# A batch-norm matmul on one core: the last column tile stored in sixteen blocks of one chunk, and the outputs of the fourth and fifth tiles moved forward

## The chip, the cores and the metric

One NeuronCore of a Trainium2 chip. The metric is the device time of one execution in microseconds (us). A profile shows one execution; its span is some 2 us shorter than the time. The granted clock in the views is the share of the full TensorE clock that was let through (1.00 is full speed). A ratio between two kernels is the mean time of one kernel's fast runs over the mean of the other's from the same rounds, so it is not quite the ratio of the medians quoted beside it.

## The reference

```python
def setup_inputs():
    batch, m, k, n = 16, 512, 1024, 768
    return {"x": randn(batch, m, k), "weight": randn(k, n),
            "gamma": ones(n), "beta": zeros(n), "eps": 1e-5}

def reference(x, weight, gamma, beta, eps):
    y = np.matmul(x, weight)
    mean = np.mean(y, axis=(0, 1), keepdims=True)
    var = np.var(y, axis=(0, 1), keepdims=True)
    y_norm = (y - mean) / np.sqrt(var + eps)
    return (gamma * y_norm + beta).astype(np.float32)
```

All is float32; y has 8192 rows and 768 columns. The statistics of a column need all its 8192 rows, so no element of a column can be stored before the last matmul of that column.

## The kernel before

The 768 columns are six tiles of 128. Tiles 0 to 2 are handled together (partly as rows, source line 179, "row matmuls" below), and tiles 3, 4 and 5 one after the other with transposed y (line 189, "y matmuls"). The text calls tiles 3, 4 and 5 the fourth, fifth and last tile. The rows are 16 chunks of 512. The program is emitted from a list of events with model times: what stands earlier in that list comes earlier in its engine's order. The engines then wait for each other by data only. TensorE writes its results to PSUM tiles; ScalarE or VectorE copies them to SBUF tiles (a "keep" where y itself is copied), and the SP queue stores output tiles to HBM by DMA.

The parts that the change touches:

```python
    def norm(nt, c, eng):              # y * scale + shift, in place, bf16, 128x512
        ...                            # ScalarE, VectorE (line 320) or GpSimd
    def turn_y(nts, m0, tiles):        # queue `tiles` transposes of 128x128 per column tile
        o_ps = psum.tile([P, tiles, len(nts), P], bf16, tag="b")
        ...
                turns.append(((nts, m0), o_ps[:, s, a], y(nt, c)[:, i * P:(i + 1) * P]))
    def turn_one():                    # one is emitted after each y matmul
        _, dst, src = turns.pop(0)
        seq(nc.tensor.transpose(dst, src, ident))
    def out_copy(nts, m0, eng, late=False):
        while any(k == (nts, m0) for k, _, _ in turns):
            turn_one()                 # what is left is emitted here, in a row
        ...                            # PSUM -> SBUF by ScalarE (line 349) or VectorE (line 351)
    def store(nts, m0, tiles): ...     # DMA to HBM from the SP queue

    def outputs(nt, t0, step):         # fourth and fifth tile: eight blocks of two chunks
        for b in range(C // 2):
            tb = t0 + step * b
            for i in range(2):
                at(tb - 1.4 + 0.5 * i, norm, nt, 2 * b + i, "act" if tb < tr + 2.0 else "dve")
            at(tb, turn_y, (nt,), 2 * b * CH, 2 * RT)
            at(tb + 2.2, out_copy, (nt,), 2 * b * CH, "act")
            at(tb + 2.3, store, (nt,), 2 * b * CH, 2 * RT)

    def last_outputs(nt, t0):          # nine blocks: 1, 1, then 2 chunks each
        blocks = [((0,), "v", "act"), ((1,), "v", "act"), ((2, 3), "gg", "dve"), ((4, 5), "vv", "act")]
        blocks += [((c, c + 1), "vv", "dve" if c % 4 == 2 else "act") for c in range(6, C, 2)]
        ...
    for nt in range(GA, NT):
        for c in range(EARLY, C):
            for jws in halves:
                unit(nt, c, MM_US / 2 + (0.12 if nt == GA else 0.17), jws)   # eight y matmuls a chunk
        at(pe + 0.55, finish, nt)      # aggregate, sqrt, reciprocal, scale, shift
        if nt == GA:
            outputs(nt, S + 40.0, 2.2)
        elif nt < NT - 1:
            outputs(nt, max(pe + 4.0, S + 55.0), 2.0)
        else:
            last_outputs(nt, pe + 3.0)
```

Of the kernel before, what the change touches and what calls it, by code (L numbers as in the profile page):

```python
# [10 lines left out]
def kernel(  # L11
# [36 lines left out]
    CH = 512  # L48
    RT = CH // P
    C = M // CH  # L50
# [312 lines left out]
    def at(t, fn, *args):  # L363
        events.append((t, len(events), fn, args))
# [6 lines left out]
    for kind, n, *n1 in order:  # L371
# [8 lines left out]
        m0 = n * rows  # L380
# [15 lines left out]
    pe = 0.0  # L396
# [12 lines left out]
    def unit(nt, c, span, jws=range(JW)):  # L409
        nonlocal pe  # L410
        pe = max(pe, arrive[c * RT + RT - 1])
        at(pe, mm, nt, c, jws)
        pe += span
        if jws[-1] == JW - 1:
            at(pe + 0.2, bn, nt, c)
            at(pe + 1.0, keep, nt, c)
# [12 lines left out]
    pe = max(pe, arrive["w", 2])  # L429
# [17 lines left out]
    S = pe  # L447
# [21 lines left out]
    def outputs(nt, t0, step):  # L469
# [7 lines that stand above are left out]

    def last_outputs(nt, t0):

        blocks = [((0,), "v", "act"), ((1,), "v", "act"), ((2, 3), "gg", "dve"), ((4, 5), "vv", "act")]  # L480
        blocks += [((c, c + 1), "vv", "dve" if c % 4 == 2 else "act") for c in range(6, C, 2)]
        tb = t0
        for chunks, by, eng in blocks:
            for c, who in zip(chunks, by):
                at(tb - (1.2 if who == "v" else 2.0), norm, nt, c, "dve" if who == "v" else "pool")
            m0, tiles = chunks[0] * CH, len(chunks) * RT
            at(tb, turn_y, (nt,), m0, tiles)
            at(tb + 0.5, out_copy, (nt,), m0, eng, True)
            at(tb + 0.6, store, (nt,), m0, tiles)
            tb += 0.5 * len(chunks)  # L490

    halves = [range(JW // 2), range(JW // 2, JW)]
    for nt in range(GA, NT):
        for c in range(EARLY, C):
            for jws in halves:
                unit(nt, c, MM_US / 2 + (0.12 if nt == GA else 0.17), jws)
        at(pe + 0.55, finish, nt)
        if nt == GA:
            outputs(nt, S + 40.0, 2.2)
        elif nt < NT - 1:  # L500
            outputs(nt, max(pe + 4.0, S + 55.0), 2.0)
        else:
            last_outputs(nt, pe + 3.0)

# [38 lines left out]
```

## Time and profile before

| | before |
|---|---|
| time, median of the first 3 runs | 223.67 us (223.32 to 224.12) |
| profiled span | 221.4 us |
| TensorE busy | 91% |
| last y matmul starts | 198.6 us |
| DMA engines full | 203.2 to 218.2 us |
| last data packet ends | 220.0 us |

One more view serves as a ruler: the list of one source line's instructions, which gives the first and last start of the row matmuls and of the y matmuls.

```profile
L179 PE MATMUL y_ps<-w_sb,xT_sb x320: 323/326/326, 24.8 to 120.0; 128*128 128x384 bf16 x160
L189 PE MATMUL y_ps<-xT_sb,w_sb x540: 273/387/632, 10.2 to 198.6; 128*128 128x512 bf16 x172, 128*128 128x256 bf16 x8
```

From 120.0 (last row matmul) to 198.6 (last y matmul) is 78.6 us, called the **stream**; from there to the end of the span is 22.8 us, the **tail**. The tail has the hand-over (the last statistics, the constants, the first blocks) and then the **drain**, in which the DMA engines are busy without a break.

### The profile page before, as it was taken

Reading aid. Unit: us, or ns where it says so; the run is one execution under the profiler, and the core shown is the slowest. Engines: PE = TensorE matmul, PEld = TensorE weight load, DVE = VectorE, ACT = ScalarE, POOL = GpSimd, SP = SyncE. Lnnn points to the kernel's source line nnn. Section 1 sums busy time; section 2 is a strip of 40 time slices with the busy share of each in tenths; the row PEclk is TensorE's granted clock in tenths of the full one; section 3 lists DMA queues with packets and bytes.
Section 4 is the critical chain, followed back from the end, with each engine's and each line's share of the span. In section 5 each row is a group of like instructions: output and inputs, shape, how many; then the busy total and the mean of one; then the engine's idle time right before and its main releaser. Section 6 shows DMA issues by size and latency. Waiting matters only on the chain.

```text
span 221.4 us, 3354 instructions
## 1 busy us (share of the span) xinstructions
PE 201.3 (91%) x1166; PEld 104.0 (47%) x1166; DVE 150.9 (68%) x260; ACT 117.5 (53%) x207; POOL 122.5 (55%) x145
## 2 busy tenths in 40 slices
PE   7669999999999999999999999999999999996510
PEld 3344555444545456465465544454444555555300
DVE  3222878897778888888634389778977568558930
ACT  2001553533554556465466217878879976858500
POOL 8897595964678689655069005996999300003000
PEclk9979999999999999999999999999999999997965
DMA  5999999999999999990000002898899998978995
GB/s 60 176 197 175 196 196 196 197 197 196 194 190 196 197 195 196 196 182 4 0 0 4 0 0 104 320 337 312 310 340 341 330 272 254 302 228 260 346 347 164
DMA packets 70049, 43.74 MB, mean 198 GB/s; under 512 B 3984, under 2 KB 69520, under 8 KB 70032
## 3 DMA queue, kind: packets, MB, share of 16 engines
q0 software_dynamic: 34624, 18.36, 60.6%
q1 hardware_dynamic: 35408, 25.18, 35.2%
q8 instruction: 9, 0.15, 0.3%
q14 instruction: 8, 0.07, 0.1%
HBM read 36.71 MB, written 25.17 MB: 280 GB/s over the span
## 4 chain that ended last, share of the span: by engine, by line
PE 84%; DMA 4%; DVE 3%; ACT 2%; issue 1%; POOL 1%; DVEq 0%; ACTq 0%; POOLq 0%
PE y_ps L189 52%; PE y_ps L179 23%; PE o_ps L336 7%; DMA ring<-in_x_dram 4%; DVE o_sb L351 1%; ACT o_sb L349 1%; POOL ring L155 1%; DVE y_sb L320 1%; ACT y_sb L315 1%; PE a_ps L262 1%; PE tot_ps L225 1%; ACT ring L349 0%; DVE xT_sb L167 0%; DVE stats L295 0%; ACT y_sb L298 0%
## 5 line engine op out<-in xcount | busy, mean ns | idle before, releaser
L189 PE MATMUL y_ps<-xT_sb,w_sb 128*128 128x512 bf16 (+1 forms) x540 | 133.0, 386 | 3.8 <-DVE xT_sb L167 1.9
L189 PEld LDWEIGHTS <-w_sb 128*128 128x128 bf16 x540 | 52.0, 97 | 69.7 <-issue 5.8
L295 DVE BATCH_NORM_STATS2 stats<-y_ps 128x6 f32<-128x512 f32 x66 | 45.0, 689 | 32.0 <-PE y_ps L189 31.8
L298 ACT CAST y_sb<-y_ps 128x512 bf16<-128x512 f32 x66 | 38.7, 586 | 52.2 <-DVE stats L295 49.5
L155 POOL DMA_DIRECT2D ring<-in_x_dram x72 | 45.3, 635 | 14.1 <-DVE xT_sb L167 7.4
L179 PE MATMUL y_ps<-w_sb,xT_sb 128*128 128x384 bf16 x320 | 53.1, 326 | 0.0
L336 PE MATMUL o_ps<-ident,y_sb 128*128 128x128 bf16 x264 | 45.5, 227 | 4.9 <-DVE y_sb L320 2.6
L167 DVE STREAM_TRANSPOSE xT_sb<-ring 128x1024 f32<-128x1024 f32 (+1 forms) x34 | 39.3, 1167 | 12.1 <-DMA ring<-in_x_dram 12.1
L205 POOL TENSOR_TENSOR sum<-sum,sq_sb 128x384 f32<-128x384 f32 x32 | 32.1, 1003 | 22.5 <-ACT sq_sb L201 21.3
L276 POOL TENSOR_TENSOR ring<-ring,sum 128x768 f32<-128x768 f32 x20 | 36.1, 1843 | 15.2 <-DVE ring L270 14.9
L179 PEld LDWEIGHTS <-xT_sb 128*128 128x128 bf16 x320 | 31.3, 98 | 21.6
L349 ACT CAST ring<-o_ps 128x1024 f32<-128x1024 bf16 (+1 forms) x28 | 25.8, 925 | 12.6 <-ACT y_sb L298 5.9
L208 DVE TENSOR_TENSOR sum<-y_ps,sum 128x384 f32<-128x384 f32 x40 | 21.8, 546 | 13.7 <-ACT sq_sb L201 13.1
L336 PEld LDWEIGHTS <-y_sb 128*128 128x128 bf16 x264 | 22.9, 101 | 9.9 <-DVE y_sb L320 6.0
L201 ACT ACTIVATE sq_sb<-y_ps 128x384 f32<-128x384 f32 x40 | 19.5, 493 | 13.1 <-PE y_ps L179 10.7
L214 ACT CAST y_sb<-y_ps 128x384 bf16<-128x384 f32 x40 | 19.0, 476 | 6.4 <-DVE sum L208 6.2
L270 DVE TENSOR_TENSOR ring<-y_sb,a_ps 128x768 f32<-128x768 bf16 x20 | 18.7, 938 | 0.0
L320 POOL TENSOR_SCALAR y_sb<-y_sb,scale,shift 128x512 bf16<-128x512 bf16 x2 | 1.7, 846 | 28.0 <-DVE shift L309 28.0
L315 ACT ACTIVATE y_sb<-y_sb,shift,scale 128x512 bf16<-128x512 bf16 x21 | 16.3, 816 | 0.0
L320 DVE TENSOR_SCALAR y_sb<-y_sb,scale,shift 128x512 bf16<-128x512 bf16 x43 | 16.1, 424 | 0.0
L148 PE MATMUL idle_ps<-idle_sb 128*128 128x512 bf16 x26 | 7.1, 441 | 1.2 <-DVE idle_sb L99 1.2
L142 POOL DMA_DIRECT2D w_sb<-in_weight_dram x12 | 6.1, 513 | 0.5 <-issue 0.2
(47 smaller groups left out, 36.3 us busy)
## 6 DMA issues: line engine op xcount, KB each, us to landing
ring<-in_x_dram POOLq DMA_DIRECT2D x56, 256.0 KB, 8.7
out_dram<-ring SPq DMA_DIRECT2D x32, 384.0 KB, 3.3
out_dram<-ring SPq DMA_DIRECT2D x16, 512.0 KB, 3.0
out_dram<-o_sb SPq DMA_DIRECT2D x7, 512.0 KB, 5.9
ring<-in_x_dram POOLq DMA_DIRECT2D x16, 128.0 KB, 5.2
w_sb<-in_weight_dram POOLq DMA_DIRECT2D x8, 96.0 KB, 4.5
w_sb<-in_weight_dram POOLq DMA_DIRECT2D x4, 192.0 KB, 5.1
out_dram<-o_sb SPq DMA_DIRECT2D x2, 256.0 KB, 4.7
```

The lines of the kernel that those rows point to most:

```text
L155: seq(nc.gpsimd.dma_start(x_bf[32 * i:32 * i + 32], src[:, :, KQ * i:KQ * (i + 1)]))
L167: seq(nc.vector.transpose(dst[:, half, :, jw0:jw1], src[:, :, jw0:jw1]))
L179: seq(nc.tensor.matmul(y_ps, xT[c][:, jw, s * P:(s + 1) * P, e], w_sb[:, jw, e, 0:NA], start=(jw == 0 and e == 0), stop=(jw == JW - 1 and ...
L189: seq(nc.tensor.matmul(y_ps, w_sb[:, jw, e, nt * P:(nt + 1) * P], xT[c][:, jw, q0 * QR:q1 * QR, e], start=(jw == 0 and e == 0 and q0 == 0) ...
L205: seq(eng.tensor_add(acc, acc, py.pop(("sq", c, s))))
L208: seq(nc.vector.tensor_add(sum1, py["row", c, s][:, 0:NA], sum1))
L276: seq(nc.gpsimd.tensor_add(o_sb, o_sb, sum1[:, None, :].to_broadcast([P, 2, NA])))
L295: seq(nc.vector.bn_stats(stats[:, nt, i, :], py[nt, c]))
L298: seq(nc.scalar.copy(y(nt, c), py.pop((nt, c))))
L320: seq((nc.vector if eng == "dve" else nc.gpsimd).tensor_scalar(y(nt, c), y(nt, c), scale[:, nt:nt + 1], shift[:, nt:nt + 1], op0=ALU.mult, ...
L336: seq(nc.tensor.transpose(dst, src, ident))
L349: seq(nc.scalar.copy(o_sb, src))
```

## The change

The intent: the fifth tile's outputs should be out of the way when the last tile is finished, and the last tile should leave in small equal blocks, with VectorE only normalising and ScalarE only copying. GpSimd has no part in it any more.

```diff
     def last_outputs(nt, t0):
 
-        blocks = [((0,), "v", "act"), ((1,), "v", "act"), ((2, 3), "gg", "dve"), ((4, 5), "vv", "act")]
-        blocks += [((c, c + 1), "vv", "dve" if c % 4 == 2 else "act") for c in range(6, C, 2)]
-        tb = t0
-        for chunks, by, eng in blocks:
-            for c, who in zip(chunks, by):
-                at(tb - (1.2 if who == "v" else 2.0), norm, nt, c, "dve" if who == "v" else "pool")
-            m0, tiles = chunks[0] * CH, len(chunks) * RT
-            at(tb, turn_y, (nt,), m0, tiles)
-            at(tb + 0.5, out_copy, (nt,), m0, eng, True)
-            at(tb + 0.6, store, (nt,), m0, tiles)
-            tb += 0.5 * len(chunks)
+        for c in range(C):
+            tb = t0 + 0.6 * c
+            at(tb - 1.2, norm, nt, c, "dve")
+            at(tb, turn_y, (nt,), c * CH, RT)
+            at(tb + 0.5, out_copy, (nt,), c * CH, "act", True)
+            at(tb + 0.6, store, (nt,), c * CH, RT)
 ...
         if nt == GA:
-            outputs(nt, S + 40.0, 2.2)
+            outputs(nt, S + 39.5, 2.0)
         elif nt < NT - 1:
-            outputs(nt, max(pe + 4.0, S + 55.0), 2.0)
+            outputs(nt, pe + 4.6, 1.85)
```

## The prediction

> **What bounds the kernel now.** I read the page first: TensorE busy 91%, and in slices the DMA row says that the last three slices are nothing but transfers. So I cut the span into windows: the stream of matmuls with its transposes, the hand-over, the drain, what is left.
>
> ```profile
> 166.00:199.00 33.00, 33.00 (x239) 17.75 (x237) 21.30 (x47) 26.10 (x37) 7.53 (x5) 1.00 0.90 288
> 199.00:203.20 4.20, 2.31 (x27) 1.70 (x25) 3.91 (x10) 3.65 (x6) 1.68 (x2) 0.85 0.81 243
> 203.20:218.20 15.00, 5.16 (x57) 3.70 (x54) 8.38 (x16) 3.98 (x5) 0.00 (x0) 0.73 1.14 344
> 218.40:219.90 1.50, 0.00 (x0) 0.00 (x0) 0.00 (x0) 0.00 (x0) 0.00 (x0) 0.50 0.08 23
> ```
>
> The columns are the window and its length, busy us of TensorE, its weight load, VectorE, ScalarE, GpSimd, then granted clock, DMA share and GB/s. TensorE has no gap up to 199.0, and the list of waits shows none for it from 120 to 199.1. From 203.2 to 218.2 the DMA engines run full at 344 to 348 GB/s and no compute engine does. 15.0 us x 344 GB/s is 5.16 MB; the last column tile is 8192 x 128 x 4 = 4.19 MB. The other MB is two blocks (0.52 MB each) of the fifth tile, as the timeline of the hand-over shows:
>
> ```profile
> 199.12 1.01 ACT L349 CAST ring<-o_ps 128x1024 f32<-128x1024 bf16 x1 [0.75 <-ACT y_sb L298]
> ...
> 201.23 1.93 ACT L349 CAST ring<-o_ps 128x1024 f32<-128x1024 bf16 x2
> 201.42 2.22 DVE L320 TENSOR_SCALAR y_sb<-y_sb,scale,shift 128x512 bf16<-128x512 bf16 x4
> 201.49 1.68 POOL L320 TENSOR_SCALAR y_sb<-y_sb,scale,shift 128x512 bf16<-128x512 bf16 x2 [27.96 <-DVE shift L309]
> ...
> 203.04 1.09 ACT L349 CAST o_sb<-o_ps 128x512 f32<-128x512 bf16 x2
> 203.67 12.07 SPq L354 DMA_DIRECT2D out_dram<-o_sb  x9
> ```
>
> ScalarE still copies two fifth-tile blocks ("ring") at 201.2 to 203.2, so the first last-tile copy ("o_sb") waits until 203.04 although its constants are ready at 201.4.
>
> The fourth window is odd: 1.5 us at 23 GB/s, a sixteenth of 347 or so: one DMA engine alone finishes late. The queue list of 202.4 to 204.6 shows why, I think:
>
> ```profile
> q1 hardware_dynamic: 1038, 0.52, 79.0%
> q8 instruction: 1, 0.02, 4.5%
> ```
>
> One 16 KB fetch of instructions lies just at the start of the drain (in the trace it starts at 202.87 and takes 1.59 us), and until about 204.5 the share is 1.08 instead of 1.15, again one sixteenth less. The engine that fetched starts 1.5 us late and, every engine having an equal share, ends 1.5 us late. So the end is **last matmul, then finish chain, then drain, then that straggler, then 1.5 us** of completion (219.9 to 221.4).
>
> **What the Trainium skill says.** "DMA: Bandwidth & Descriptors", Specifications: HBM gives a core about 358 GB/s; the trace's 347 in the drain agrees, so the drain can't be made faster, only started earlier and freed of other data. "Runtime: NRT & Kernel Launch", Instruction fetch mechanics: instructions are refilled in 16 KiB blocks (256 instructions) by a DMA queue of the sequencer, a cost "mostly hidden". The trace shows such packets (about 20 us apart lately), but the one at 202.87 seems not hidden. "GPSIMD Engine Reference", Specifications: GpSimd shares SBUF interfaces with VectorE in a 2-port mode; the trace agrees: four norms take 2.22 us (0.56 each) beside GpSimd's two and 1.38 us (0.35 each) later. "TensorE: Matmul & The Clock Gate", Part 1: an idle array falls to half clock; the windows show 0.50 from 202 to 205, transposes then at about 0.12 us.
>
> **The change part by part.** The order of instructions of the two builds shows what moves. Both have 64 + 17 against 64 transposes after the last y matmul: before, 17 of the fifth tile come after it, now none.
>
> 1. *Transposes before the last matmul.* Eight matmuls alone take 8 x 0.226 = 1.81 us (chain of waits: seven in 1.58); with eight transposes between, they follow each other at 0.2815, so a transpose costs 0.056. 17 x 0.056 = **+0.95 us** on TensorE's path: last matmul from 198.99 to 199.94.
>
> 2. *A stall at the fourth tile.* Its steps shrink too (2.2 to 2.0, start 0.5 earlier). The order shows its first transposes now after five matmuls of a unit, three matmuls (0.7 us) earlier than before. In the trace that transpose would be due at about 168.5, but the ScalarE norm that makes its data is the first of these two, ending about 169.1:
>
> ```profile
> 168.30 1.52 ACT L315 ACTIVATE y_sb<-y_sb,shift,scale 128x512 bf16<-128x512 bf16 x2
> 169.73 0.57 ACT L298 CAST y_sb<-y_ps 128x512 bf16<-128x512 f32 x1
> 170.19 1.53 ACT L315 ACTIVATE y_sb<-y_sb,shift,scale 128x512 bf16<-128x512 bf16 x2
> 171.62 0.57 ACT L298 CAST y_sb<-y_ps 128x512 bf16<-128x512 f32 x1
> 172.08 1.02 ACT L349 CAST ring<-o_ps 128x1024 f32<-128x1024 bf16 x1
> 172.99 1.53 ACT L315 ACTIVATE y_sb<-y_sb,shift,scale 128x512 bf16<-128x512 bf16 x2
> ```
>
> ScalarE is packed there, so TensorE waits: 0.6 us, and perhaps 0.1 for the norms at 172.99: **+0.7 us**, the term I trust least (0 to 1). Last matmul then 200.64.
>
> 3. *Overlap of fourth and fifth tile.* Three units now carry 52 transposes: TensorE 24 x 0.226 + 52 x 0.056 = 8.3 us; ScalarE 7 copies x 1.01 + 3 keeps x 0.59 = 8.8 us; seven blocks of 0.52 MB are 3.7 MB, 10.6 us of DMA at 347, which the ring of six blocks and the next, lighter units absorb. ScalarE falls behind by half a us; eight PSUM banks at three allocations per 2.7 us allow 7 us of life, and I count at most 6. **0**, with little to spare.
>
> 4. *Finish chain.* Before, 199.02 to 201.42, with one fifth-tile norm (0.31) between statistics and aggregation. That norm is now earlier: 2.10 us instead of 2.41, **-0.3 us**. Norms start at 202.75.
>
> 5. *First block.* Norm 0.35 (GpSimd is out of it), four transposes at half clock 0.48, copy about 0.55, some 0.1 of hand-overs: first store at about 204.2. From issue to the first byte takes 0.9 (the issue at 200.16 moves bytes from 201.1), so the drain starts at **205.2** instead of 203.2.
>
> 6. *Drain.* Only 4.19 MB: at 347 GB/s **12.1 us** (before 15.0). Each chunk is 0.76 us of DMA, against 0.35 of VectorE, at most 0.48 of TensorE, and about 0.58 of ScalarE (1.09 for two, beside GpSimd): supply outruns it. 512 KB or 256 KB blocks have the same 512-byte rows, so the rate should hold; the queue's issues (0.37 to 0.52 us each when not held back) fit. VectorE's four copies (4 x 1.22) vanish, which was hidden and is worth nothing. End of drain 217.3, was 218.2.
>
> 7. *Straggler.* The count of TensorE instructions ahead of the last tile is the same (row 2179 in both), so the fetch should come again about 1 us after its first transpose: 203.1 + 0.9 = 204.0, ending 204.9 at the undisturbed 0.95 us, just before the drain. Then no engine is late: **-1.5 us**. Last byte 217.3, was 219.9.
>
> Sum: 217.3 - 219.9 = -2.6 us, which gives 221.1; I put 221.2, since the fetch may still touch the drain.
>
> **Rivals.** *A stall takes the place of the hidden drain*: with ScalarE packed at 168 to 175 and again in the overlap, TensorE could lose 1.5 to 2 us instead of 0.7; then 222.0 to 222.5. For it: 26.1 of 33 us of ScalarE busy already. Against it: TensorE never waited there before. *The straggler stays*: the fetch is tied to something else and still hits the drain; then 222.6. For it: its margin above is 0.3 us. *No stall at all*: my placing of the transpose is 0.6 us off; then 220.4. *The small blocks starve the queue* because ScalarE alone copies (0.7 instead of 0.58 with waits): 16 x 0.7 = 11.2 us, still below 12.1; it would need 0.85 to cost 1.5 us. Unlikely.
>
> **Range and chances.** The plausible combinations run from 220.4 (no stall, no straggler) to 222.6; with 0.3 us of spread in the runs (223.32 to 224.12) I take 219.9 to 222.7. Faster by over 2% would need under 219.2: 1.3 us of gain beyond the best combination, 0.05. Slower by over 2% needs a lasting stall of over 4 us in the overlap: 0.02.
>
> **What would show it.** After the change: windows with the DMA share at or near 0 just before the drain; a drain of 12.1 us at 347 GB/s with no second phase at 23 GB/s; an instruction packet before the first store's bytes; the last y matmul at about 200.6, with 0.6 us of TensorE idle near 168.5 released by ScalarE's norm (if not, 199.9); GpSimd idle after 174; norms of 0.35. I am wrong if the first store comes later than 204.8, if the straggler is there again, or if DMA rate falls with 256 KB blocks.

## More of the kernel before

What lies ahead of 120 us, called the load phase (the loading of x and what runs beside it), differs between executions of one kernel by more than a microsecond. The stream and the tail do not contain it, so they show small effects that the total hides.

## The result, and the profile after

The changed kernel took 220.78 us (median of 4 runs, 220.42 to 221.63) against 223.56 us (4 runs). The ratio is 0.9878, with a 95% interval of 0.9842 to 0.9913. Two later sets of 6 runs gave 0.9914 each time. So the gain is between 0.9% and 1.2%, and inside the predicted range each time.

The windows of the changed kernel, cut as those of before (columns as there): the hand-over, the drain, what is left.

```profile
199.90:204.70 4.80, 2.08 (x22) 1.93 (x22) 4.39 (x14) 2.25 (x6) 0.00 (x0) 0.81 0.28 85
204.70:217.10 12.40, 3.36 (x46) 3.19 (x44) 2.77 (x9) 6.45 (x14) 0.00 (x0) 0.78 1.13 338
217.10:218.60 1.50, 0.00 (x0) 0.00 (x0) 0.00 (x0) 0.00 (x0) 0.00 (x0) 0.50 0.00 0
```

The drain is 12.4 us long instead of 15.0, and its data are the last tile's alone. After it nothing moves: the phase at 23 GB/s is gone, and only the 1.5 us of completion remain. Before the drain the DMA engines now stand nearly idle; the fifth tile's last bytes arrive at 201.3. The timeline of the hand-over shows one copier and one normaliser:

```profile
202.22 5.25 DVE L320 TENSOR_SCALAR y_sb<-y_sb,scale,shift 128x512 bf16<-128x512 bf16 x16
202.68 5.21 PEld L336 LDWEIGHTS <-y_sb 128*128 128x128 bf16 x64 [3.22 <-DVE y_sb L320]
202.68 5.38 PE L336 MATMUL o_ps<-ident,y_sb 128*128 128x128 bf16 x64 [2.71 <-DVE y_sb L320]
203.21 7.93 ACT L349 CAST o_sb<-o_ps 128x512 f32<-128x512 bf16 x16 [1.08 <-PE o_ps L336]
203.82 10.19 SPq L354 DMA_DIRECT2D out_dram<-o_sb  x16
```

Sixteen norms take 5.25 us (0.33 each), sixteen copies 7.93 us (0.50 each): both faster than the DMA, which needs 0.76 us for a chunk. The list of TensorE's waits and the ruler show what was paid for it:

```profile
PE o_ps L336 <- DVE y_sb L320: 2.7, 1, 2.7
PE o_ps L336 <- ACT y_sb L315: 0.5, 1, 0.5
...
L179 PE MATMUL y_ps<-w_sb,xT_sb x320: 323/326/326, 24.0 to 119.2; 128*128 128x384 bf16 x160
L189 PE MATMUL y_ps<-xT_sb,w_sb x540: 273/387/390, 10.1 to 199.6; 128*128 128x512 bf16 x172, 128*128 128x256 bf16 x8
```

(The waits are us in total, times, longest; the 2.7 us is the hand-over itself.) The stream is 80.4 us, 1.8 longer than before; the tail is 19.0 us, 3.8 shorter. Together 99.4 instead of 101.4: the last two tiles' stage gained 2.0 us. The two profiled spans differ by 2.8 us; the remaining 0.8 us is the load phase, which in this profile ended at 119.2 instead of 120.0 with the same instructions in it. That is luck, and no profile shows whether the other runs of the first set had it too. The later sets, with a gain of 1.9 us each (0.0086 of 223.5), agree with the stage.

### The profile page after: what moved, and what is told of

It reads as the page before. It is cut to its first block, busy times and chain, and to the rows that moved or that the text cites. A ratio compares the mean times of both kernels' runs of the same rounds, so it can differ in the third digit from the quotient of the medians.

```text
span 218.6 us, 3380 instructions
## 1 busy us (share of the span) xinstructions
PE 199.5 (91%) x1166; PEld 103.7 (47%) x1166; DVE 146.7 (67%) x258; ACT 121.2 (55%) x218; POOL 120.8 (55%) x143
## 4 chain that ended last, share of the span: by engine, by line
PE 82%; DMA 5%; ACT 4%; POOL 3%; issue 1%; DVE 1%; ACTq 0%; POOLq 0%
PE y_ps L189 51%; PE y_ps L179 24%; PE o_ps L336 6%; ACT o_sb L349 3%; DMA w_sb<-in_weight_dram 2%; DMA ring<-in_x_dram 2%; POOL w_sb L142 2%; POOL ring L155 1%; PE a_ps L262 1%; PE tot_ps L225 1%; ACTq L533 0%; ACT ring L349 0%; ACT y_sb L315 0%; DVE stats L295 0%; DVE mv L302 0%
## 5 line engine op out<-in xcount | busy, mean ns | idle before, releaser
L189 PEld LDWEIGHTS <-w_sb 128*128 128x128 bf16 x540 | 51.3, 96 | 68.5 <-issue 5.3
L336 PE MATMUL o_ps<-ident,y_sb 128*128 128x128 bf16 x264 | 43.1, 230 | 3.4 <-DVE y_sb L320 2.7
L276 POOL TENSOR_TENSOR ring<-ring,sum 128x768 f32<-128x768 f32 x20 | 36.1, 1833 | 15.3 <-DVE ring L270 15.1
L201 ACT ACTIVATE sq_sb<-y_ps 128x384 f32<-128x384 f32 x40 | 19.5, 494 | 11.1 <-PE y_ps L179 8.9
L214 ACT CAST y_sb<-y_ps 128x384 bf16<-128x384 f32 x40 | 19.1, 478 | 8.7 <-DVE sum L208 8.6
L148 PE MATMUL idle_ps<-idle_sb 128*128 128x512 bf16 x26 | 7.6, 462 | 1.2 <-DVE idle_sb L99 1.2
L349 ACT CAST o_sb<-o_ps 128x512 f32<-128x512 bf16 x16 | 7.9, 673 | 1.1 <-PE o_ps L336 1.1
```

What stands on the lines that cost most here:

```text
L189: seq(nc.tensor.matmul(y_ps, w_sb[:, jw, e, nt * P:(nt + 1) * P], xT[c][:, jw, q0 * QR:q1 * QR, e], start=(jw == 0 and e == 0 and q0 == 0) ...
L201: seq(nc.scalar.activation(sq_sb, py["row", c, s][:, 0:NA], AF.Square))
L276: seq(nc.gpsimd.tensor_add(o_sb, o_sb, sum1[:, None, :].to_broadcast([P, 2, NA])))
L349: seq(nc.scalar.copy(o_sb, src))
```

## The experiments

Eleven runs. The ruler for all of them, in us, from one profile each:

| version | stream | tail | both | ratio to before (95%) |
|---|---|---|---|---|
| before | 78.6 | 22.8 | 101.4 | 1 |
| changed, first set | 80.4 | 19.0 | 99.4 | 0.9878 (0.9842 to 0.9913) |
| changed again | 80.4 | 19.2 | 99.6 | 0.9914 (0.9882 to 0.9946) |
| changed again | 80.5 | 19.1 | 99.6 | 0.9914 (0.9894 to 0.9934) |
| only the last tile | 78.6 | 22.7 | 101.3 | 1.0014 (0.9981 to 1.0046) |
| only the fourth and fifth tile | 80.4 | 19.5 | 99.9 | 0.9905 (0.9868 to 0.9943) |
| changed, fourth tile back | 79.6 | 19.5 | 99.1 | 0.9906 (0.9860 to 0.9953) |
| the same again | 79.6 | 19.5 | 99.1 | 0.9881 (0.9858 to 0.9903) |
| before, fetch earlier | 78.6 | 21.3 | 99.9 | 0.9932 (0.9889 to 0.9974) |
| changed, fetch later | 80.4 | 20.8 | 101.2 | 0.9979 (0.9937 to 1.0021) |
| changed, fetch earlier | 80.4 | 18.9 | 99.3 | 0.9905 (0.9870 to 0.9940) |
| fourth tile back, idle matmuls | 79.6 | 18.8 | 98.4 | 0.9856 (0.9822 to 0.9890) |
| the same again | 79.5 | 18.8 | 98.3 | 0.9860 (0.9834 to 0.9886) |

### Which part of the change does it

The control, the changed kernel without an edit:

> The changed kernel once more, as the control for the runs beside it. Ratio to the kernel before 0.988 (0.985 to 0.991); 0.7 to 0.9 us of TensorE lost near 167 to 173 to ScalarE's norms; no second phase of the drain at 23 GB/s.

It came out at 0.9914, a little above what I wrote and at the upper end of the first set's interval (0.9913); stream and tail repeat to 0.2 us.

Only the last tile (the changed kernel with the old times for the two other tiles):

```diff
-            outputs(nt, S + 39.5, 2.0)
+            outputs(nt, S + 40.0, 2.2)
...
-            outputs(nt, pe + 4.6, 1.85)
+            outputs(nt, max(pe + 4.0, S + 55.0), 2.0)
```

> Only the first part of the change: the last tile in sixteen blocks of one chunk; fourth and fifth tile as before. Theory (the gain is the fifth tile leaving the drain, and the fetch of instructions leaving it): 17 transposes and two fifth-tile blocks still lie behind the last matmul, the drain still carries 5.2 MB from about 203.2, the fetch still falls into it; ratio to before 0.996 to 1.003. Rival (smaller blocks and ScalarE alone copying start the drain earlier and end it smoother): most of the gain, ratio 0.988 to 0.993.

Ratio 1.0014. The sixteen blocks alone gain nothing: stream and tail are those of before. The run with the fourth tile back (below) differs from this one only in the line of the fifth tile, and has 0.9906 and 99.1 us against 101.3: that one line makes the gain.

Only the other two tiles (the kernel before with the two new lines, the reverse of this edit):

> Only the second part: fourth and fifth tile further forward; the last tile in nine blocks, as before. Theory: nearly the whole gain, ratio 0.987 to 0.991, drain of 4.2 MB in 12.1 to 12.4 us, fetch of instructions before it, perhaps 0.2 us worse than both parts because GpSimd slows the first norms to 0.56 us. Rival (the sixteen blocks matter, the larger ones starve the queue at the start): ratio 0.994 or more, with gaps in the DMA share after the first store.

Ratio 0.9905, as good as the changed kernel within the intervals: the other two tiles' lines give the gain without the sixteen blocks. (The rival's 0.994 lies at the edge of the interval, 0.9943; the stretches decide, 99.9 us against 101.4.) The tail is 0.3 to 0.5 us longer than the changed kernel's, where I had written perhaps 0.2, and the drain takes 12.9 us (206.1 to 219.0), where I had written 12.1 to 12.4. The rival's sign is there too: for 0.5 us from 206.9 the DMA share is 0.11. But this gap lies ahead of the second store, which is one chunk in both kernels, so the larger blocks don't make it. GpSimd does slow the first norms, as expected:

```profile
203.66 2.21 DVE L320 TENSOR_SCALAR y_sb<-y_sb,scale,shift 128x512 bf16<-128x512 bf16 x4
203.74 1.67 POOL L320 TENSOR_SCALAR y_sb<-y_sb,scale,shift 128x512 bf16<-128x512 bf16 x2 [29.44 <-DVE shift L309]
```

Four norms in 2.21 us are 0.55 each, against 0.33. Yet the first store comes no later than in the changed kernel (4.15 us after the last y matmul started, against 4.14 to 4.35). The second is issued 0.70 us after the first, not 0.49, and its issue then takes 1.08 us, until 0.44 us after a fetch of instructions has ended. So most of the longer tail goes with the fetch, below; what GpSimd adds, one profile does not separate.

### The wait that the fourth tile brings

```diff
-            outputs(nt, S + 39.5, 2.0)
+            outputs(nt, S + 40.0, 2.2)
```

> The changed kernel with the fourth tile's outputs put back to their times before (start 40.0, step 2.2). Theory (TensorE waits 0.7 to 0.9 us for ScalarE's norms because the fourth tile starts 0.5 us too early): that wait is gone, last y matmul 0.7 to 0.9 us nearer to the tile's start, ratio to the changed kernel 0.996, to before 0.984. Rival (the wait comes back elsewhere, in the longer overlap of fourth and fifth tile where ScalarE has 4 blocks more to copy): same as the changed kernel, 0.988, with TensorE waiting on ScalarE at 180 to 192.

The total missed what I expected (0.9906 instead of 0.984), and the profiled execution was the slowest of its six (223.54 us; its load phase ended at 122.7). But the stream is 79.6 us, 0.8 shorter, and the wait on ScalarE's norm is gone from the list (120 to 206 us), which has one line left, the hand-over:

```profile
PE o_ps L336 <- DVE y_sb L320: 2.7, 1, 2.7
```

The longer overlap brought no new wait. So I ran it again, with the changed kernel and the last version on the same chip.

> The changed kernel a third time, so that the last two versions can be set against it on one chip. Ratio to before 0.988 to 0.992; 80.4 us from the last row matmul to the last y matmul, 19.0 to 19.3 from there to the end.

> The fourth tile's outputs at their old times, once more: in its first profile the fetch of instructions happened to collide with the first stores, and that profile was of its slowest execution. Theory: 79.6 us of matmul stream again (the wait of 0.8 us gone), tail 19.0 to 19.5 by how the fetch falls, so 0.5 to 0.8 us less than the changed kernel of this call. Rival (the 0.8 us come back in the tail): 99.4 us or more in both stretches together, total the same as the changed kernel.

The changed kernel came out as expected (0.9914, 80.5 and 19.1). With the fourth tile back it is again 79.6, and a tail of 19.5. Both together are 99.1 instead of 99.6: 0.5 of the 0.8 us arrive. (The total is 0.9967 of the changed kernel's, means 221.12 and 221.86 us, a difference of 0.7.) The other 0.3 us go with the second store, whose issue takes longer here (1.07 and 1.27 us against 0.74 to 0.97 in the three profiles of the changed kernel). What holds it is the next question.

### The fetch of instructions

In the kernel before, one DMA engine ended 1.5 us late, and the prediction put that down to a 16 KB fetch of instructions. In its trace 112 to 142 pairs of weight load and matmul lie between one 16 KB fetch and the next, 128 on average, and in all runs the last one starts after 1096 to 1118 weight loads. So I took the fetches to follow the count of pairs: some pairs more or fewer at the start of the program should shift all of them and touch nothing else.

The kernel before, with 40 pairs more (the waking matmuls that fill the wait for the first load):

```diff
-    WAKE = 26
+    WAKE = 20
...
         for _ in range(WAKE):
             seq(nc.tensor.matmul(idle_ps, idle_sb[:, 0:P], idle_sb, start=True, stop=True))
+        for _ in range(46):
+            seq(nc.tensor.matmul(idle_ps[:, 0:P], idle_sb[:, 0:P], idle_sb[:, 0:P], start=True, stop=True))
```

> The kernel before, with the waking matmuls recast as 20 long and 46 short ones: 40 more pairs of TensorE instructions ahead of everything, so each 16 KB fetch falls 40 pairs earlier; nothing else moves. Theory (the engine that ends 1.5 us late is the one that fetched at the start of the drain): the last fetch falls at about 197 to 199, the phase at 23 GB/s is gone, and from the last y matmul to the end it takes 21.3 us instead of 22.8; ratio to before 0.993 (0.990 to 0.996). Rival (one engine is slow by itself): 22.8 us and a ratio of 1.000, with the phase still there.

The fetch fell at 196.3, a little earlier than expected. The stream stayed at 78.6, and the tail became 21.3 us, as expected to the tenth. Its windows of hand-over, drain and rest:

```profile
199.90:204.40 4.50, 2.42 (x32) 1.69 (x30) 3.83 (x10) 3.57 (x6) 1.63 (x2) 0.99 0.78 236
204.40:219.60 15.20, 6.38 (x54) 5.21 (x52) 8.63 (x16) 4.05 (x6) 0.05 (x1) 0.50 1.14 344
219.60:221.20 1.60, 0.00 (x0) 0.00 (x0) 0.00 (x0) 0.00 (x0) 0.00 (x0) 0.50 0.03 7
```

The drain is as long as before (15.2 us: it still carries two blocks of the fifth tile), but the phase at 23 GB/s after it is gone. The ratio is 0.9932. That the late engine was late because of the fetch is shown by this run: only the waking matmuls were changed, and what came out of place was the fetch.

The opposite: the changed kernel with 20 pairs fewer, so that the fetch falls into the drain.

```diff
-    WAKE = 26
+    WAKE = 6
```

> The changed kernel with 6 waking matmuls instead of 26: 20 pairs fewer, so the last fetch falls some 1.7 us later, into the drain. Theory: a phase of 1.0 to 1.5 us at 23 GB/s comes back at the end, and last y matmul to end takes 20.2 to 20.7 us instead of the 19.0 to 19.2 of the changed kernel. Rival: 19.1, no such phase. The colder start can move the whole by up to 1 us either way, so the verdict is taken from that stretch and not from the total; total 0.990 to 0.999.

The tail grew to 20.8 us, a little more than I had written, and the total to 0.9979, which gives back most of the gain. But the phase at 23 GB/s at the end is only 0.8 us long. The rest was lost inside the drain, in a way that I had not expected:

```profile
207.20:209.40 2.20, 2.20 (x29) 1.52 (x30) 2.20 (x8) 2.20 (x5) 0.00 (x0) 1.00 1.14 338
209.40:210.40 1.00, 1.00 (x13) 0.65 (x12) 0.56 (x2) 1.00 (x4) 0.00 (x0) 1.00 0.12 27
210.40:220.60 10.20, 0.02 (x1) 0.00 (x0) 0.00 (x0) 3.35 (x7) 0.00 (x0) 0.68 1.11 335
220.60:221.40 0.80, 0.00 (x0) 0.00 (x0) 0.00 (x0) 0.00 (x0) 0.00 (x0) 0.50 0.08 23
```

For 1.0 us in the middle nearly all DMA engines stand still (share 0.12), although ScalarE has copied blocks ready. The timeline of the store queue in that run shows one issue that takes 2.25 us, where its neighbours take 0.5:

```profile
207.86 2.25 SPq L354 DMA_DIRECT2D out_dram<-o_sb  x1
```

The fetch in this run lasts from 208.00 to 209.71. The issue ends 0.4 us after it. The same interval appears where a fetch meets the first stores: the second store's issue ends 0.43 us after the end of the fetch in the changed kernel's first profile (204.62, 205.05), and 0.43 to 0.46 in its two others, in both runs with the fourth tile back and in the run of only the two tiles. So a fetch seems to do two things: it holds its own engine, and it can hold a store's issue until 0.4 us after its own end; if too little is queued by then, the other fifteen engines run dry. In the kernel before, an issue was held as well (203.67, for 1.72 us), but blocks of the fifth tile were still queued and the DMA engines went on (342 GB/s from 204.5 to 206), so only the first effect shows as lost time.

Two limits. Not every issue during a fetch is held: the changed kernel's first store (203.82, 0.37 us) is not, nor is a store of the fifth tile in the run above (196.94, 0.37 us). And issues are also long with no 16 KB fetch near, as the one at 215.76 in this run (1.08 us). So the times alone would not show it; the next run, which moves the fetch away from the second store, does. How the issue comes to wait is not visible in a trace.

The changed kernel with the 40 pairs more of the first edit:

> The changed kernel with the same recast waking matmuls as the other run (40 pairs more), nothing else. Theory (the fetch at the first stores stretches the second issue and so delays the drain): fetch near 198, second issue about 0.4 us, last y matmul to end 18.6 instead of 19.1; ratio to before 0.986 to 0.989. Rival (the second issue is always long): 19.1 us.

The fetch fell at 196.4, again earlier than expected. The second issue took 0.44 us, as expected. Here it is beside that of the changed kernel's first profile (line 356 is line 354 of the other):

```profile
204.31 0.74 SPq L354 DMA_DIRECT2D out_dram<-o_sb  x1
205.86 0.44 SPq L356 DMA_DIRECT2D out_dram<-o_sb  x1
```

But the tail is 18.9, not 18.6: the collision had cost only 0.1 to 0.3 us in the changed kernel, less than I had thought. The stretch from the first store's issue to the end of the span shows it best: 14.7 us here, 14.8 where the second issue takes 0.74 or 0.76 us, 15.0 at 0.97, and 15.1 and 15.3 at 1.07 and 1.27 with the fourth tile back. The ratio, 0.9905, does not tell this from the changed kernel.

The two runs with the fetch moved also say what the change is worth apart from it. With the fetch out of the way in both kernels, stream and tail together take 99.9 us before and 99.3 us after (mean times 221.9 and 221.3 us): 0.6 us. So of the 2.0 us that the change gains, about 1.4 come from the fetch no longer falling into the drain, and 0.6 from the rest. (These are one profile each and means of six runs; the intervals of the two ratios overlap.)

### A version that beats both

The fourth tile back at its old times, and 28 short idle matmuls after the last y matmul, while TensorE waits anyway. They are meant to keep its clock up, and to make the fetch fall ahead of the first stores.

```diff
+    def fill(n):
+        idle_ps = psum.tile([P, CH], f32, tag="b")
+        for _ in range(n):
+            seq(nc.tensor.matmul(idle_ps[:, 0:P], ident, ident, start=True, stop=True))
...
-            outputs(nt, S + 39.5, 2.0)
+            outputs(nt, S + 40.0, 2.2)
...
+            at(pe + 3.2, fill, 28)
             last_outputs(nt, pe + 3.0)
```

> The changed kernel with the fourth tile back at its old times and 28 short idle matmuls of TensorE after the last y matmul, which keep its clock up and pull the fetch of instructions ahead of the first stores. Theory: 79.6 us from the last row matmul to the last y matmul (80.4 in the changed kernel), then 18.3 to 18.7 to the end (19.0 to 19.2): the second store is issued in about 0.4 us instead of 0.74 to 1.07. Ratio to before 0.983 (0.980 to 0.986). Rival (stretching of the second issue has nothing to do with the fetch): 19.1 us, ratio 0.986 to 0.988.

> The version with the fourth tile back and the 28 idle matmuls, once more, against the changed kernel on the same chip. Theory: 98.4 us in both stretches together against 99.5, so a total 0.9 to 1.3 us below the changed kernel (ratio of the two 0.994 to 0.996) and 0.985 of before. Rival (the earlier difference was the luck of the load phase): ratio of the two within 0.002 of 1.

Both runs agree: stream 79.6 and 79.5, tail 18.8 (0.1 more than the upper end of what I wrote), the second issue 0.43 and 0.44 us, the granted clock 1.00 through the first transposes. The ratio to before is 0.9856 and 0.9860; to the changed kernel 0.9937 (means 220.46 and 221.86 us). That is 1.4 us, a little more than I wrote, of which 1.3 show in stream and tail. The edit does two things to the tail. The fetch now falls at 197.9, and from the first store's issue to the end it is 14.7 us, as in the run with the fetch earlier. The clock matters less: the first store is issued 4.14 or 4.15 us after the last y matmul in all profiles of kernels with sixteen blocks and the fifth tile moved in which the granted clock was 1.00 over the first 1.5 us of transposes. These include one of the changed kernel and one with the fourth tile back, without idle matmuls; it is 4.24 us at a clock of 0.56 and 4.35 at 0.50. So the clock's share is 0.1 to 0.2 us, in those executions where it was low.

## Why the prediction was right, point by point

The number (221.2) lies between the three medians of the changed kernel (220.78, 221.59, 221.80), and the predicted gain of 1.1% between the measured 0.9% and 1.2%. By its steps:

1. *Transposes ahead of the last matmul, +0.95.* Measured 1.0: the stream without the stall is 79.6, that of before 78.6.
2. *The stall at the fourth tile, +0.7.* Measured 0.8 (80.4 against 79.6). It was where it was said to be, counted from the last row matmul: this profile runs 0.8 us ahead. In the changed kernel's timeline the first of those transposes waits for ScalarE's norm:

```profile
166.52 1.29 PE L189 MATMUL y_ps<-xT_sb,w_sb 128*128 128x512 bf16 x5
168.33 0.23 PE L336 MATMUL o_ps<-ident,y_sb 128*128 128x128 bf16 x1 [0.52 <-ACT y_sb L315]
168.40 0.39 PE L189 MATMUL y_ps<-xT_sb,w_sb 128*128 128x512 bf16 x1
...
172.62 0.39 PE L189 MATMUL y_ps<-xT_sb,w_sb 128*128 128x512 bf16 x1
173.02 0.23 PE L336 MATMUL o_ps<-ident,y_sb 128*128 128x128 bf16 x1
```

   There are 0.52 us at 168, and another 0.2 at 172.6, where the next transpose follows 0.40 us after its matmul instead of 0.23. The "perhaps 0.1" of the prediction was the second; the list of waits names no releaser for it, but ScalarE's first norm of that pair ends at about 172.9.
3. *The overlap of fourth and fifth tile, 0.* No wait of TensorE there, neither in the changed kernel nor with the fourth tile back.
4. *Finish chain, -0.3.* From the start of the last statistics to the first norm it is 2.21 us (200.01 to 202.22) against 2.40 before: -0.2.
5. *First block.* From the first norm to the first store 1.60 us (202.22 to 203.82), predicted about 1.5; from there to the first byte 0.91, predicted 0.9.
6. *Drain 12.1.* Measured 12.4: the second store was held by the fetch. In the last version it is 12.3 (204.3 to 216.6), so the fetch is not all of the 0.3; I did not look for the rest. The rate held with 256 KB blocks (344 to 346 GB/s in stretches of 1 to 2 us after 206). That the drain can't be made faster than this, as the prediction says, no run here tested; the cited figure agrees with the measured rate, which does not prove it a limit.
7. *The straggler, -1.5.* Shown by the run with the fetch moved in the kernel before (tail 22.8 to 21.3). In the changed kernel the fetch lies from 203.66 to 204.62, just ahead of the first data at 204.73. (By the same reading it began at 202.93 in the kernel before, not at 202.87 as the prediction has it.) The margin was even thinner than said (0.1 us instead of 0.3; in the third profile of this kernel the fetch ended 0.1 us after the first data), and the run with the fetch in the drain shows what lies behind it: 1.7 us.

The sum, -2.6, was somewhat too large: stream and tail together gained 1.8 to 2.0. The terms of +0.95 and +0.7 came out 0.15 larger together, those of the chain, the first block and the drain some 0.5 smaller. The first comparison hides that, because its profile had 0.8 us of luck in the load phase. More than half of the predicted sum was the fetch (-1.5), and the runs agree (about 1.4 of 2.0 us). The rival of a stall of 1.5 to 2 us and that of a queue starved by ScalarE did not come about. The one that the straggler stays came about in a form not foreseen: not as a late engine but as a held store, at 0.1 to 0.3 us.

What stays open: why the second store is held 0.1 to 0.5 us longer with the fourth tile back (five profiles of it and the changed kernel are too few), what made the granted clock at the first transposes low in some executions of one kernel and full in others, and why the load phase of one kernel ends anywhere from 119.2 to 120.3 us.

## What to carry to other kernels

When a kernel ends in a drain at full DMA rate, ask first what else is in that drain. Here it was the fifth tile's last megabyte and a fetch of instructions. Moving the fifth tile took the drain clear of both and made the whole gain of 2.0 us, but 1.4 of it came from the fetch and only 0.6 from the megabyte, after what the move costs. The size and number of the blocks gave nothing. Work that is moved forward is paid where it lands, here 1.0 us of TensorE and 0.8 us of waiting for a packed ScalarE, and the second part was avoidable. And look at the instruction fetches in the DMA view: forty pairs of idle instructions at the start decided whether one of them cost 1.5 us.

## What the Trainium skill lacked or had wrong

- "Runtime: NRT & Kernel Launch", Instruction fetch mechanics, calls the cost of crossing a 16 KiB boundary mostly hidden. That can hold for TensorE itself (its list of waits in the kernel before is empty from 120 to 199 us, with fetches in it), but not for the stores: one fetch cost 1.5 us of 223 when it met a drain (tail 22.8 against 21.3 us with the fetch moved), and 1.7 us when it met the few stores queued in the changed kernel (20.8 against 19.1). The 16 KB fetches of these runs took 0.9 to 2.0 us each.
- No page that I read says that a store's issue can be held while an instruction fetch is under way. Here an issue that takes about 0.4 to 0.6 us in the changed kernel took 0.74 to 2.25 us, ending 0.4 us after the fetch did, and in one run the other engines ran dry for 1.0 us.
